# Layer 1's projection as seven products of quarters with spilled results, and one layout of buffers for a two-layer encoder

## The chip, the cores and the metric

The kernel runs on one core of a Trainium2 chip. The metric is device time in microseconds (us) of one execution. The engines are TensorE (PE: matmuls, with its weight loads shown as PEld), VectorE (DVE), ScalarE (ACT), GpSimd (POOL) and SyncE (SP, which here only issues DMAs). Sixteen DMA engines carry what SP and GpSimd issue.

## What is computed

Two post-norm layers on x of 512 tokens x 2048 features, in float32. Layer 1 is gated grouped-query attention with 16 query heads and 4 key/value heads of 128:

```python
proj = h @ w_in                                   # 2048 -> 5120: q 2048, k 512, v 512, g 2048
q = apply_rope(rms_norm(q, q_gain), cos, sin) * (A_HEAD_DIM ** -0.5)
k = apply_rope(rms_norm(k, k_gain), cos, sin)
...
p = jax.nn.softmax(s, axis=-1)                    # s = q k^T, per head, all 512 keys
...
return (o * jax.nn.silu(g)) @ w_out               # o = p v
```

Layer 2 is gated retention with 8 heads (q and k of 256, v and g of 512, so 2048 -> 12288): rope on q and k, scores times a decay by distance in both directions, times v, a norm per head, times silu(g), and an output projection 4096 -> 2048. After each layer x becomes layer_norm(ALPHA * x + y) with gain and bias.

## The kernel before

**Split products.** Every float32 operand is split into a rounded high part and a low part (`split`, L117: ACT copies the high part to fp32r, L118; DVE subtracts for the low part, L119). `mm3` (L261) is one product of 128x128 by 128x512 in three matmuls, high x high, high x low, low x high (L263 to L265). TensorE's order is the program's order. The other engines' orders come from the framework's planner, which schedules by data, buffers and its own costs.

**Weights** come in chunks of 128 x 1024 (512 KB), listed in `order` (L144). `load_chunk` (L233) issues the load through SP into a `raw` buffer and splits it; `next_chunk` (L250) keeps AHEAD = 2 chunks made ahead of the one in use. A `Stream` (L267) is a generator of products; `pump(us)` emits products worth so much by the constant MM3 (L274), so other work is placed between them by hand.

**Layer 1** (L586 to L605) goes group by group, four groups of four query heads with one k/v head. k and v of a group come from `kv_stream` (L474) as products of 256 columns, q from `q_stream` (L487) through `n_form` (L291), the gate from `gate_stream` (L496) through `t_form` (L307), which leaves features on the partitions. `q_group` does RMS norm and rope (`rms_open` L441, `rope` L452; two of its products are on GpSimd, L468) and turns q; `att_group` (L517) does scores, softmax (L527 to L532), transposes of the weights (L396), values, and the gate. The filler between those is the output projection of the group before (`out_proj`, L329), then the gate and the next k and v.

**Between the layers** `out_proj_last` (L343) works token tiles (0, 1), then 2, then 3; `norm_1` (L664) norms each and stores it to DRAM; `turn_1` (L672) transposes it and applies gain and bias on ACT. It is overlapped with products 1 and 2 of layer 2's first block (L805 to L813). Then the pools of layer 1 are closed and others opened (L815 to L817).

**Layer 2's projection** is done by seven products in place of eight: x is cut in quarters (token halves by feature halves), a block of weights (2048 x 1024) in four, and sums of quarters are multiplied (`form` L684 for x; `block_sum` L202 for the weights, whose sums DVE makes, L212). A product has four chunks; each chunk feeds four split products; a block is 7 x 4 x 4 = 112 split products, 336 matmuls. `evacuate` (L740) combines results, `deliver` (L722) applies rope or silu and stores to DRAM through GpSimd. There are 12 blocks, three for a pair of heads.

**Layer 2's heads.** `Head.run` (L896) does a head's scores and values, with the last block or the output projection of the head before as filler. After head 0 the pools change again (L987), and `residual` (L958) loads the normed layer-1 result and its gain and bias through GpSimd, multiplies on DVE and adds on GpSimd (L969, L970). `out_proj_last` with resident weights and `norm_2` (L927) end the kernel.

Of the kernel before, what the change touches and what calls it, by code (L numbers as in the profile page):

```python
# [26 lines left out]
N_G = R_HEADS // 2 * 3  # L27
CH = 1024
AHEAD = 2
ACC = 5  # L30
MM3 = 0.64
LOOK = 2
Q_HEAD = 7.0
Q_EACH = 4.5
A_HEAD = 2.0
EACH = 3.0
EACH_FIRST = 2.0
EACH_LAST = 2.0
PART = 0.5
T_HEAD = (4.0, 1.5, 4.0, 5.0)  # L40
T_EACH = 1.2
S_EACH = 1.2
S_TAIL = 2.0
O_EACH = 2.5
O_TAIL = 3.5
# [3 lines left out]
def encoder_trunk_kernel(  # L49
# [10 lines left out]

    nc = tc.nc
# [9 lines left out]
    class Pools:  # L71


        def __init__(self, **bufs):
            self.stack = ExitStack()
            for n, b in bufs.items():
                setattr(self, n, self.stack.enter_context(tc.tile_pool(name=n, bufs=b, reuse_waits="tile")))

        def close(self):
            self.stack.close()  # L80

    ph = Pools(hp=24, tmp=6, rp=3, yp=1)
# [7 lines left out]
    def bank():  # L90
        return psum.tile([P, 512], F32, tag="acc", name=nm("acc"))

    def bank2(name):
        return psum.tile([P, 512], F32, tag="att", name=nm(name), bufs=8 - ACC)

    def half(name, dt=F32R, tag="half"):
        return ph.hp.tile([P, 512], dt, tag=tag, name=nm(name), bufs=24 if tag == "half" else 4)

    def pair(name, tag="half"):
        return half(name + "h", F32R, tag), half(name + "l", F32R, tag)  # L100

    def temp(name):
        return ph.tmp.tile([P, 512], F32, tag="temp", name=nm(name))

    def unit(name, dt=F32R, pool=None):
        return (pool or xp).tile([P, 4, 512], dt, tag="x", name=nm(name))

    def small(name, n=1):
        return tiny.tile([P, n], F32, tag=name, name=nm(name))

    def v4(x):
        return x.rearrange("p (n d) -> p n d", d=P)

# [8 lines left out]
    def whole(hi, lo):  # L122
        return [(hi, lo, slice(0, 2))]

    def dest_stream(i):
        return whole(*[wp.tile([P, 2, 512], F32R, tag=n, name=nm(n)) for n in ("whi", "wlo")])

    def dest_halves(i):
        r = []
        for k in range(2):  # L130
            h, l = pair("ow", "sg" if i == n_l1 - 1 else "half")
            r.append((h.unsqueeze(1), l.unsqueeze(1), slice(k, k + 1)))
        return r

    resident = {}

    def dest_x(c, kc):
        def d(i):
            if kc == 0:
                resident[c] = [unit("wres") for _ in range(2)]  # L140
            return whole(*[m[:, 2 * kc:2 * kc + 2] for m in resident[c]])
        return d

    order = []  # L144

    def add(src, dest=dest_stream):
        order.append((src, dest))

    def add_n(w, u):
        for kc in range(8):  # L150
            add(w[u, kc])

    def add_t(w, u):
        for hf in range(2):
            add(w[u, hf])

    def add_o(w, u):
        for c in range(4):
            for kc in range(2):
                add(w[u, c, kc])  # L160

    def add_o_last(w, u, dest):
        for c in range(4):
            for kc in range(2):
                add(w[u, c, kc], dest(c, kc))

    for kc in range(4):
        add(a["wa_kv"][0, kc])
    for g in range(GROUPS):
        add_n(a["wa_q"], g)  # L170
        if g > 0:
            add_o(a["wa_o"], g - 1)
        for j in range(HPG):
            add_t(a["wa_g"], 4 * g + j)
        if g < GROUPS - 1:
            for kc in range(4):
                add(a["wa_kv"][g + 1, kc])
    add_o_last(a["wa_o"], GROUPS - 1, lambda c, kc: dest_stream if 2 * c + kc < 3 else dest_halves)
    n_l1 = len(order)
    FIRST = (1, 2, 5, 6, 3, 7, 4)  # L180
    PRODUCTS = (1, 5, 6, 3, 7, 2, 4)
    for g in range(N_G):
        for p in FIRST if g == 0 else PRODUCTS:
            for c in range(4):
                order.append((g, p, c))
        if g == 0:
            n_open = n_l1 + 8
    for h in range(R_HEADS - 1):
        add_o(a["wr_o"], h)
    add_o_last(a["wr_o"], R_HEADS - 1, dest_x)  # L190

    ready = []
    taken = [0]

    def raw_load(src):
        raw = ph.rp.tile([P, 2, 512], F32, tag="raw", name=nm("raw"))
        nc.sync.dma_start(out=raw.rearrange("p k n -> p (k n)"), in_=src)
        return raw

    held = {}  # L200

    def block_sum(g, p, c):  # L202

        def quarter(kh, nb):
            return raw_load(a["wr_in"][g, 2 * kh + nb, c])

        def keep(key, kh, nb):
            held[key, c] = quarter(kh, nb)
            return held[key, c]

        def onto(x, y):
            nc.vector.tensor_add(x, x, y)  # L212
# [882 lines left out]
```

## Time and profile before

| | |
|---|---|
| three runs | 2265.59, 2267.30, 2267.55 us; median 2267.3 |
| profiled execution | 2264.06 us, span of instructions 2262.3 us |
| PE, PEld busy | 2188.5 us (97%), 1830.5 us (81%) |
| DVE, ACT, POOL busy | 1590.7 us (70%), 956.8 us (42%), 204.0 us (9%) |
| TensorE instructions | 10448 |
| DMA | 300.66 MB, mean 133 GB/s |

The span runs from the first to the last instruction. Busy times of PE overlap, since matmuls are pipelined: a busy PE is not a full PE. A group's row gives line, engine, operation, output and inputs, shapes and count, then the busy time in us and the mean ns of one, then the idle time before it and what ended that. A row of the chain gives start, length, engine and line of one step. A row of the DMA issues gives count, size and the median us from issue to landing.

### The profile page before, as it was taken

The page shows a single profiled execution, that of the slowest core. Times are in us where ns is not written, and L with a number is a line of the kernel's source. Part 1 is how long each engine was busy: PE and PEld are TensorE (multiplying, and loading weights), DVE is VectorE, ACT ScalarE, POOL GpSimd, SP SyncE. Part 2 cuts the span into 40 slices and gives each one's busy share as a digit, 9 for nine tenths or more (in the row PEclk, how much of TensorE's full clock was granted, in tenths as well). Part 3 has the DMA queues.
Part 4 walks back from the last instruction along what each step waited for, and adds up shares of the span by engine and source line. Part 5 has one row for each costly group of instructions (what it writes and reads, how often), then busy time and mean ns, then how long its engine had stood idle before and what let it go on. Part 6 is the DMA issues. An engine that isn't in the chain of part 4 may idle for free.

```text
span 2262.3 us, 27514 instructions
## 1 busy us (share of the span) xinstructions
PE 2188.5 (97%) x10448; PEld 1830.5 (81%) x10448; DVE 1590.7 (70%) x2419; ACT 956.8 (42%) x1399; POOL 204.0 (9%) x247
## 2 busy tenths in 40 slices
PE   9999999999999979999999999999997699999997
PEld 8898888889888768888888888888886488888886
DVE  5565654655567897867787788778786766666667
ACT  4353243244245744444444444444464333333331
POOL 1201100200200000000000000000003400000004
PEclk9999999999999989999999999999999799999999
DMA  7312312322323364554465445545555433333332
GB/s 279 94 47 84 94 65 84 91 68 67 104 73 94 121 226 161 189 179 142 143 204 159 131 160 187 168 136 180 186 178 175 140 112 124 128 112 126 106 122 75
DMA packets 83557, 300.66 MB, mean 133 GB/s; under 512 B 10337, under 2 KB 11617, under 8 KB 81121
## 3 DMA queue, kind: packets, MB, share of 16 engines
q1 hardware_dynamic: 73440, 263.25, 36.0%
q0 software_dynamic: 9984, 35.66, 4.5%
q8 instruction: 82, 1.34, 0.2%
q14 instruction: 51, 0.41, 0.1%
HBM read 265.31 MB, written 33.55 MB: 132 GB/s over the span
## 4 chain that ended last, share of the span: by engine, by line
PE 91%; DVE 4%; POOL 2%; DMA 1%; issue 1%; ACT 1%; SPq 0%; POOLq 0%; DVEq 0%; ACTq 0%
PE acc L263 26%; PE acc L265 26%; PE acc L264 26%; PE tr L396 3%; PE o L263 2%; PE o L265 2%; PE o L264 2%; PE s L263 1%; PE s L264 1%; PE s L265 1%; POOL y L970 1%; DMA ln_bias<-in_ln_bias_dram 1%; DVE wlo L246 1%; DVE f L119 0%; DVE q_x L446 0%
## 5 line engine op out<-in xcount | busy, mean ns | idle before, releaser
L118 ACT CAST whi<-raw 128x1024 fp32r<-128x1024 f32 (+1 forms) x340 | 356.2, 1048 | 434.2 <-PE acc L265 393.2
L263 PE MATMUL acc<-whi,f 128*128 128x512 f32 x1344 | 526.1, 391 | 12.5 <-ACT whi L118 12.1
L264 PE MATMUL acc<-wlo,f 128*128 128x512 f32 x1344 | 523.9, 390 | 0.8 <-DVE wlo L119 0.7
L265 PE MATMUL acc<-whi,f 128*128 128x512 f32 x1344 | 523.7, 390 | 0.0
L119 DVE TENSOR_TENSOR wlo<-raw,whi 128x1024 fp32r<-128x1024 f32 (+1 forms) x340 | 409.5, 1212 | 154.0 <-ACT whi L118 149.8
L246 DVE TENSOR_TENSOR wlo<-raw,whi 128x512 fp32r<-128x512 f32 x324 | 215.2, 695 | 213.1 <-ACT whi L244 212.8
L244 ACT CAST whi<-raw 128x1024 fp32r<-128x1024 f32 x162 | 170.2, 1051 | 374.9 <-PE acc L265 192.2
L263 PEld LDWEIGHTS acc<-whi,f 128*128 128x128 f32 x1344 | 252.7, 188 | 65.1 <-ACT whi L118 12.5
L264 PEld LDWEIGHTS acc<-wlo,f 128*128 128x128 f32 x1344 | 252.8, 188 | 53.4 <-DVE wlo L119 1.9
L265 PEld LDWEIGHTS acc<-whi,f 128*128 128x128 f32 x1344 | 252.7, 188 | 52.6
L212 DVE TENSOR_TENSOR raw<-raw,raw 128x1024 f32<-128x1024 f32 x192 | 231.9, 1221 | 36.6 <-DMA raw<-in_wr_in_dram 35.5
L263 PE MATMUL acc<-whi,xT 128*128 128x256 f32 (+1 forms) x512 | 175.1, 342 | 4.9 <-ACT xT L118 4.9
L263 PE MATMUL acc<-whi,og 128*128 128x512 f32 x448 | 175.8, 392 | 0.0
L265 PE MATMUL acc<-whi,og 128*128 128x512 f32 x448 | 174.6, 390 | 0.0
L264 PE MATMUL acc<-wlo,og 128*128 128x512 f32 x448 | 174.6, 390 | 0.0
L265 PE MATMUL acc<-whi,xT 128*128 128x256 f32 (+1 forms) x512 | 173.6, 339 | 0.6 <-DVE xT L119 0.6
L264 PE MATMUL acc<-wlo,xT 128*128 128x256 f32 (+1 forms) x512 | 173.2, 338 | 0.0
L327 DVE TENSOR_TENSOR y<-acc,y 128x512 f32<-128x512 f32 x160 | 107.6, 686 | 26.7 <-PE acc L265 26.1
L263 PEld LDWEIGHTS acc<-whi,xT 128*128 128x128 f32 x512 | 98.3, 192 | 16.9 <-ACT xT L118 4.9
L265 PEld LDWEIGHTS acc<-whi,xT 128*128 128x128 f32 x512 | 98.2, 192 | 11.1 <-DVE xT L119 1.0
L264 PEld LDWEIGHTS acc<-wlo,xT 128*128 128x128 f32 x512 | 98.3, 192 | 10.1
L263 PE MATMUL acc<-xT,whi 128*128 128x512 f32 x256 | 102.6, 401 | 0.0
(184 smaller groups left out, 3355.8 us busy)
## 6 DMA issues: line engine op xcount, KB each, us to landing
raw<-in_wr_in_dram SPq DMA_DIRECT2D x248, 512.0 KB, 4.3
raw<-in_wr_o_dram SPq DMA_DIRECT2D x64, 512.0 KB, 3.6
raw<-in_wa_q_dram SPq DMA_DIRECT2D x32, 512.0 KB, 3.5
raw<-in_wa_g_dram SPq DMA_DIRECT2D x32, 512.0 KB, 3.5
raw<-in_wa_o_dram SPq DMA_DIRECT2D x32, 512.0 KB, 3.5
qkD<-qkT POOLq DMA_DIRECT2D x32, 256.0 KB, 5.4
vD<-t POOLq DMA_DIRECT2D x32, 256.0 KB, 5.0
raw<-qkD SPq DMA_DIRECT2D x16, 512.0 KB, 3.8
```

Source lines behind the costliest of these rows:

```text
L118: nc.scalar.copy(hi, src)
L119: nc.vector.tensor_sub(lo, src, hi.bitcast(F32))
L212: nc.vector.tensor_add(x, x, y)
L244: nc.scalar.copy(hi, raw[:, k])
L246: nc.vector.tensor_sub(lo[:, j], raw[:, k.start + j], hi[:, j].bitcast(F32))
L263: nc.tensor.matmul(ps, sh, mh, start=start, stop=False, skip_group_check=go_on)
L264: nc.tensor.matmul(ps, sh, ml, start=False, stop=False, skip_group_check=go_on)
L265: nc.tensor.matmul(ps, sl, mh, start=False, stop=stop, skip_group_check=go_on)
L327: nc.vector.tensor_add(yc, ps, yc)
L396: nc.tensor.transpose(out=b[:, tcols(i)], in_=src[:, tcols(i)], identity=ident)
L970: nc.gpsimd.tensor_add(y[:, t, cs], y[:, t, cs], gb[1])
```

## The change

Layer 1 becomes two stages. Its input projection is done like layer 2's: five blocks of two 512-column pieces, each by seven products of quarters, with all results spilled to DRAM. Attention then loads q, k, v and gate back, with the last block and later the output projections as filler. In the diff below, classes and functions that only changed their form are left out.

```diff
+A_COLS = ((("v", 0), ("g", 0)), (("g", 1), ("k", 0)), (("q", 0), ("q", 1)), (("q", 2), ("g", 2)), (("q", 3), ("g", 3)))
+FETCH = 3
-MM3 = 0.64
+MM3 = 0.68
+ORDER = (1, 5, 6, 3, 7, 2, 4)
...
-    xp = ctx.enter_context(tc.tile_pool(name="xp", bufs=8))
+    xp = ctx.enter_context(tc.tile_pool(name="xp", bufs=32))
+    rp = ctx.enter_context(tc.tile_pool(name="rp", bufs=9))
+    tmp = ctx.enter_context(tc.tile_pool(name="tmp", bufs=13))
-    psum = ctx.enter_context(tc.tile_pool(name="psum", bufs=ACC, space=bass.MemoryType.PSUM))
+    psum = ctx.enter_context(tc.tile_pool(name="psum", bufs=8, space=bass.MemoryType.PSUM))
...
+    def onto(x, src):
+        nc.gpsimd.dma_start(out=x, in_=src, accum_op=ALU.add)
...
+        def fetch(self, p, c):
...
+            if p == 1:
+                g[1 if self.first else "v", c] = raw_load(q(11))
+            elif p == 2:
+                g[2, c] = raw_load(q(21))
+            elif p == 6:
+                g[3, c] = raw_load(q(22))
+            elif p == 5 and self.first:
+                g["v", c] = raw_load(q(11))
+                onto(g["v", c], q(12))
+        def make(self, p, c):
...
+            if p == 6:
+                nc.vector.tensor_add(v, v, g[3, c])
+            elif p == 4 and not self.first:
+                nc.vector.tensor_add(v, v, g[2, c])
...
+        def follow(self, p, c):
...
+            if p == 1 and not self.first:
+                onto(g["v", c], q(12))
+            elif p == 3:
+                onto(g[3, c], q(12))
+            elif p == 6 and self.first:
+                onto(g["v", c], q(21))
...
+            fetch_to(len(ready) + 1 + FETCH)
+            make_chunk()
...
+        def out_proj_last(self, og):
+            for r in (0, 2):
+                for c in range(4):
...
+                            for t in (r, r + 1):
...
+    for ins, outs in ((a_in, a_out), (r_in, r_out)):
+        for b in ins[:2]:
+            b.add((1, 2))
+        for b in ins[:2]:
+            b.add((5, 6, 3, 7, 4))
+        for b in ins[2:]:
+            b.add(ORDER)
...
+        outs[-1].add(1)
...
+        for i in range(2):
-            nc.gpsimd.tensor_tensor(out=tv[:, :, :, i], in0=xv[:, :, :, 1 - i], in1=sb, op=ALU.mult)
+            nc.vector.tensor_tensor(out=tv[:, :, :, i], in0=xv[:, :, :, 1 - i], in1=sb, op=ALU.mult)
...
+    work = Stream(products(a_in[-1], x1, ORDER, ev1))
+    work.pump(31.5 * MM3)
...
+        attention(groups[g], groups[g + 1] if g + 1 < GROUPS else None, work, 2.2 if g else 2.7)
...
+    for c in range(4):
+        for t in range(NT):
+            hook(r_in[2 + c], (1, 6, 3, 2)[t], 2, residual_2, c, t)
...
-    ph.close()
-    ph = Pools(yp=1, tmp=8, rp=4)
-    residual()
+            total.load(lambda t: yD2[:, t])
...
-    nc = bacc.Bacc("TRN2", target_bir_lowering=False, num_devices=1, dynamic_dma_scratch_size=4096)
+    nc = bacc.Bacc("TRN2", target_bir_lowering=False, num_devices=1, dynamic_dma_scratch_size=2048)
```

- `Block.fetch` issues a chunk's loads FETCH chunks before it is made; `make` is its sum on DVE; `follow` is what is added to the quarter by an accumulating DMA from GpSimd (`onto`) once it is split. Of a regular block's 16 sums, eight stay on DVE and eight go to DMA; in the first two blocks of a layer four stay and twelve go to DMA.
- Both layers begin with products 1 and 2 of blocks 0 and 1, and then do the other five of each. Operand forms of x are made at hooks on chunks of those.
- Gate results now have tokens on the partitions. The reciprocal of the softmax sum is multiplied into the gate (one operation for four heads), which is then transposed (`Group.close`); the multiplication of each head's weights by it is gone.
- `out_proj_last` does token tiles 0 and 1, then 2 and 3, and streams the weights twice. Its norms come in pairs.
- `residual_2` makes the scaled residual of layer 2 during blocks 2 to 5 of its projection, 16 pieces, each loaded through SP, with two DVE operations, and stored through GpSimd; `Sum.load` loads the result (4 MB) after head 0.
- All pools live for the whole kernel; nothing is closed or opened between the stages.

More of the change, by code (lines that the diff above doesn't have):

```diff
@@ L250, in next_chunk, with fetch_to, make_chunk @@
+    def fetch_to(n):
+        while fetched[0] < min(len(order), n):
+            blk, p, c = order[fetched[0]]
+            blk.fetch(p, c)
+            fetched[0] += 1
+    def make_chunk():
+        blk, p, c = order[len(ready)]
+        raw = blk.make(p, c)
+        hi, lo = [wp.tile([P, CH], F32R, tag=n, name=nm(n)) for n in ("whi", "wlo")]
+        split(hi, lo, raw)
+        blk.follow(p, c)
+        ready.append([(half(hi, j), half(lo, j)) for j in range(2)])
     def next_chunk():
@@ L418, in start, with load_quarter @@
+    gD = [in_dram(f"gD{g}", [P, NT, 512]) for g in range(GROUPS)]
+    x1 = Operand()
+    def load_quarter(r, kh, i):
+        nc.sync.dma_start(out=x1.quarter(r, kh, i), in_=a["xq"][r, kh, i])
     def start():
[L420 to L421 removed]
+        blk = order[0][0]
+        raw = rp.tile([P, CH], F32, tag="raw", name=nm("raw"))
+        hi, lo = [wp.tile([P, CH], F32R, tag=n, name=nm(n)) for n in ("whi", "wlo")]
+        xf, (fh, fl) = x1.quarter(0, 0, 0), x1.new_form(1, 0)
@@ L507, in q_group @@
[L507 to L526 removed]
+        return dst, ss
@@ new lines, in attention @@
+            if w >= 0 and w % 2:
+                t, h = units[w]
+                g.values(h // 2, pT.pop(w))
+                if h == HPG - 1:
+                    g.weigh(t, p[w][1])
+            work.pump(each / 2)
+            if w >= 0 and w % HPG == HPG - 1:
+                g.close(w // HPG)
+    start()
+    ev1 = spill(deliver_1)
+    Stream(in_stream(a_in, x1, ev1, 1)).drain()
+    groups = [Group(g) for g in range(GROUPS)]
+    total = Sum()
+    work = Stream(products(a_in[-1], x1, ORDER, ev1))
@@ L813, in encoder_trunk_kernel @@
-    work.drain()
-    run_later(9)
-    ph.close()
-    f2 = ctx.enter_context(tc.tile_pool(name="f2", bufs=7, reuse_waits="tile"))
-    ph = Pools(rp=10, tmp=14)
-    form(5, 0)
-    form(5, 1)
-    Stream(group(0, FIRST[2:]), *[group(g) for g in range(1, N_G - 1)]).drain()
+                nc.scalar.copy(o, transpose4(m))
+                nc.gpsimd.dma_start(out=qkD[2 * pr + kind][:, :, tcols(t)], in_=v4(o))
+            turn_soon(lambda src: soon(3, put, rope_2(t, src)), t, src, own)
     def decay_strip(h):
-        st = const.tile([P, 896], F32, tag="tabs", name=nm("strip"))
+        st = const.tile([P, 1024], F32, tag="tabs", name=nm("strip"))
@@ new lines, in encoder_trunk_kernel @@
+    work = Stream(total.out_proj_last(groups[-1].out), in_stream(r_in, x2, ev2, 1))
+    work.until(lambda: 0 in total.rows)
+    norm_1(0)
+    norm_1(1)
+    work.pump(4.0)
+    for t in range(2):
+        for c in (0, 1, 2, 3):
+            turn_1(t, c)
+            work.pump(1.2)
+    work.until(lambda: 2 in total.rows)
+    norm_1(2)
+    norm_1(3)
+    work.pump(5.0)
+    for h in range(2):
+        for t in (2, 3):
+            for c in (h, h + 2):
+                turn_1(t, c)
+                work.pump(1.2)
+        x2.form(5, h)
@@ L1006, in encoder_trunk_kernel @@
-    ph.close()
+    heads[0].open()
+    work.pump(30.5 * MM3)
+    for h in range(R_HEADS):
+        if h:
+            work = Stream(total.out_proj(heads[h - 1].out, 1.0))
+        heads[h].run(work, heads[h + 1] if h + 1 < R_HEADS else None, 2.4)
+        work.drain()
+        if h == 0:
+            total.load(lambda t: yD2[:, t])
+    work = Stream(total.out_proj_last(heads[-1].out))
+    work.pump(20.0)
+    ln_params()
+    work.until(lambda: 0 in total.rows)
+    norm_2(0)
+    norm_2(1)
```

1102 lines of the change are left out of this document (482 added, 620 removed).

## The prediction

> **What bounds the kernel now.** I read the page's 40 slices first, then busy time by stretch, then the chain that ended last, then the groups of instructions by form and the DMA issues.
>
> ```profile
> span 2262.3 us, 27514 instructions
> ...
> PE   9999999999999979999999999999997699999997
> ```
>
> Of 40 slices TensorE is short of full in four: the 15th (791 to 848 us, the change of layers), two around 1700 to 1800 us, and the last. So the kernel is as long as its TensorE work plus what is lost there. The stretches (start and length; busy time with counts of PE, PEld, DVE, ACT, POOL; granted clock; DMA share; GB/s):
>
> ```profile
> 0.00:20.00 20.00, 14.53 (x93) 13.96 (x94) 12.60 (x24) 12.89 (x20) 0.20 (x4) 1.00 0.88 326
> 784.00:808.00 24.00, 7.41 (x25) 4.81 (x24) 24.00 (x32) 11.18 (x13) 1.46 (x2) 0.61 0.61 229
> 1089.00:1321.20 232.20, 232.20 (x1043) 192.45 (x1041) 182.50 (x199) 106.57 (x118) 14.54 (x24) 1.00 0.51 163
> 1739.00:1788.00 49.00, 14.35 (x43) 9.47 (x42) 34.43 (x34) 9.69 (x11) 28.96 (x21) 0.65 0.57 185
> ```
>
> Row 3 is one period of the retention projection: TensorE never stops, at clock 1.00. Rows 2 and 4 are the two places where it does: 24.00 - 7.41 = 16.6 us and 49.00 - 14.35 = 34.65 us idle, with the clock down to 0.61 and 0.65.
>
> The price of a matmul is its step in the chain, not its duration, since matmuls overlap:
>
> ```profile
> 1089.00 0.87 PE tr L396 x8
> ...
> 1321.22 0.87 PE tr L396 x8
> ```
>
> Between these lie 232.22 us, with three blocks of 336 products of 512 columns and four such runs of eight transposes. So a product costs (232.22 - 4 x 0.87) / 1008 = 0.227 us, a transpose 0.87 / 8 = 0.109 us, and a split product (three matmuls) 0.68 us; a chunk of weights feeds four of those, 2.72 us. In the k/v projection of layer 1, 256 columns wide, the chain shows
>
> ```profile
> 24.91 0.12 PE acc L263
> ```
>
> **The change part by part.** *Matmuls.* What layer 1's projection has now (one of three lines each):
>
> ```profile
> L263 PE MATMUL acc<-xT,whi 128*128 128x512 f32 x256 | 102.6, 401 | 0.0
> L263 PE MATMUL acc<-whi,xT 128*128 128x512 f32 x256 | 100.5, 392 | 0.0
> ...
> L263 PE MATMUL acc<-whi,xT 128*128 128x256 f32 x256 | 74.7, 292 | 4.9 <-ACT xT L118 4.9
> ```
>
> Removed: q and gate, 2 x 3 x 256 products of 512 columns (1536 x 0.227 = 348.5 us), and k/v, 768 x 0.12 = 92.2 us. Added: five blocks of seven products, 5 x 336 x 0.227 = 381.2 us, and 16 x 4 transposes of the gate, which now comes with tokens on the partitions, 64 x 0.109 = 7.0 us. Scores, values, the other transposes, the output projection and layer 2 keep their counts. Net -52.5 us, all on the path, since nothing but TensorE sets the pace there.
>
> *The change of layers.* Row 2 says who held TensorE: DVE is busy for 24.00 of 24.00 us. It makes most operand forms of layer 2 in one go, while only two products of one block are ready to cover that. After the change two blocks open with products 1 and 2: 32 more split products, 8 chunks x 2.72 = 21.8 us of cover, and no pool is closed in between. But the last output projection now reads its weights twice. The DVE groups and the cast:
>
> ```profile
> L119 DVE TENSOR_TENSOR wlo<-raw,whi 128x1024 fp32r<-128x1024 f32 x336 | 407.8, 1221 | 151.2 <-ACT whi L118 147.0 <-DMA raw<-in_wr_in_dram 3.5
> L118 ACT CAST whi<-raw 128x1024 fp32r<-128x1024 f32 x336 | 354.6, 1055 | 432.6 <-PE acc L265 393.2 <-issue 20.7 <-DVE raw L212 13.3
> ...
> L212 DVE TENSOR_TENSOR raw<-raw,raw 128x1024 f32<-128x1024 f32 x192 | 231.9, 1221 | 36.6 <-DMA raw<-in_wr_in_dram 35.5
> ...
> L327 DVE TENSOR_TENSOR y<-acc,y 128x512 f32<-128x512 f32 x160 | 107.6, 686 | 26.7 <-PE acc L265 26.1
> ...
> L366 DVE BATCH_NORM_STATS2 ln_st<-y 128x6 f32<-128x512 f32 x32 | 22.1, 690 | 0.7
> ```
>
> One pass over two token tiles is 8 chunks (21.8 us of TensorE) and costs DVE 8 x 1.221 + 8 x (0.686 + 0.690) = 20.8 us, before norms and turned operands, which on DVE come ahead of the next splits. Some stall must stay; I leave 8 of the 16.6 us (bounds 0 and 16.6). Gain 8.6.
>
> *Layer 2's projection to its output.* The chain through row 4:
>
> ```profile
> 1735.93 10.28 DMA ln_bias<-in_ln_bias_dram
> 1746.35 2.65 POOL y L970 x2
> 1749.56 11.13 POOL y L970 x6
> 1761.19 6.91 DMA ln_bias<-in_ln_bias_dram
> ```
>
> The residual is loaded, scaled on DVE and POOL, and only then used. The change makes it during four projection blocks: 16 pairs of DVE operations of about 0.7 us, 5.5 us a block, where row 3 shows DVE idle for 49.7 of 232.2 us. Its loads go through SP ahead of the next weights, its stores through GpSimd among the spills; both find their data ready. Only a plain load of 4 MB is left. At row 1's 326 / 0.88 = 370 GB/s that is 11.3 us, against 16 us until head 1 finishes its first output columns (4 score units of 6 x 0.227 us and 16 split products). I leave 4 us, for the buffers that come free with the last product (0 to 16). Gain 34.65 - 4 = 30.6.
>
> *DVE in layer 1.* Rope is wholly on DVE now, RMS first:
>
> ```profile
> L470 DVE TENSOR_TENSOR r_dst<-r_dst,r_sq 128x256 f32<-128x256 f32 x40 | 17.5, 468 | 2.5 <-POOL r_sq L468 2.5
> L457 DVE TENSOR_REDUCE r_ss<-r_sq 128x4 f32<-128x512 f32 x20 | 13.5, 674 | 0.0
> L469 DVE TENSOR_TENSOR r_dst<-q_x,tabs 128x256 f32<-128x256 f32 x32 | 12.7, 413 | 0.0
> ...
> L446 DVE SCALAR_TENSOR_TENSOR q_x<-acc,tabs 128x512 f32<-128x512 f32 x16 | 10.3, 684 | 6.6 <-ACT r_sq L445 6.6
> ```
>
> One tile: 0.684 + 0.674 + 4 x 0.413 + 2 x 0.468 = 3.95 us. The block of q0 and q1 delivers eight within 18 chunks: 31.6 us, with 18 splits (22.0), four sums (4.9) and four evacuations at 0.68 (2.7) 61.2 us, where TensorE needs 18 x 2.72 + 8 x 0.44 = 52.5. Two chunks made ahead are 5.4 us of lead; 3.3 are left: +3 (0 to 9).
>
> *Attention.* Two of its DVE groups now:
>
> ```profile
> L527 DVE TENSOR_REDUCE nmax<-s 128x1 f32<-128x512 f32 x64 | 44.0, 688 | 28.0 <-PE s L265 27.8
> L532 DVE TENSOR_SCALAR p<-p,rs 128x512 f32<-128x512 f32 x64 | 31.1, 486 | 2.0
> ```
>
> L532 goes (the weights are scaled through the gate). A unit then has L527 and a split of 512 columns, 0.69 as L327; a token tile has four more operations of that size. Beside the last block, group 0 runs 16 x 1.38 + 16 x 0.69 = 33.1 us of these, 20 weight splits (24.4), some six sums (7.3), four rope tiles (15.8) and six evacuations (4.1): 84.7 us. TensorE has 80 split products (54.4 us), 16 units of scores 0.68, transposes 4 x 0.109 and values 6 x 0.12 (29.4) and 8 turned tiles (3.5): 87.3. That is 97%, with order and latency on top: +4 (0 to 15; the high end takes in late PSUM banks, which now come from one pool of eight). In groups 1 to 3 the filler's chunk feeds eight split products in place of four, so DVE has room.
>
> The queues: q, gate, k and v come back through SP, ahead of the output weights; each waits for a temporary buffer, and the weights behind it have the nine raw buffers as lead. Layer 1's weight transfers grow from 80 to 116 and its spills by 40 stores and as many loads, 116 x 1.42 + 80 x 0.71 = 222 us of DMA as plain copies in some 680 us: hidden.
>
> *Sums of quarters by DMA.* Half of L212's additions go to accumulating DMAs issued by GpSimd, 512 KB each, and layer 1 adds its own. No accumulate is in the trace. The nearest rows:
>
> ```profile
> raw<-in_wr_in_dram SPq DMA_DIRECT2D x248, 512.0 KB, 4.3
> ...
> y<-yD POOLq DMA_DIRECT2D x4, 1024.0 KB, 10.7
> ```
>
> Call T the time per accumulate with all engines on it. Least: a plain copy, 524288 B / 370 GB/s = 1.42 us. Most: the slow GpSimd load, 10.7 / 2 = 5.35 us, with no overlap. The midpoint, 3.4, is what I take. Fixed latency is 4.3 - 1.42 = 2.9 us. Tightest is the first pair of blocks of each layer: 24 accumulates, 16 loads (22.7 us) and 8 spills of 256 KB (5.7) must be in within 40 chunks less a split, 108.8 - 2.3 = 106.5 us, the 2.3 being L118 and L119. So TensorE waits 24T - 78.1: 3.5 us a layer at 3.4, +7 for both. In a later block four accumulates queue between product 1 and product 5, issued 3.1 us ahead of product 1; the fourth is due 16.7 us after its start, so T up to 16.9 / 4 = 4.2 costs nothing. Queued behind a late one on GpSimd are the spills of finished tiles and RMS's power, which hold temporary buffers and only through those TensorE.
>
> The Trainium skill, "Collectives: The Full Stack", in its section on the bandwidth ceiling, says that an add in the DMA engine halves the rate because it reads two sources for each write, and that the add itself costs nothing. By it an estimate for T is 2 x 1.42 = 2.8 us, and the +7 would be 0; no run here shows it yet.
>
> *Start.* The first matmul:
>
> ```profile
> 4.88 0.58 PE L263 MATMUL acc<-whi,xT 128*128 128x256 f32 x1 [4.88 <-ACT xT L118]
> ```
>
> Until its fifth chunk the new order needs nine transfers of 512 KB: 4.72 MB at 326 GB/s is 14.5 us, with a split 16.8 and some issue time, 17.5, against 4.9 + 4 x 2.72 = 15.8 for TensorE: +2 (0 to 6).
>
> *End.* The last matmul starts at 2248.14, and DVE ends last:
>
> ```profile
> 2248.14 0.39 PE L265 MATMUL acc<-wres,og 128*128 128x512 f32 x1
> ```
>
> ```profile
> 2258.27 0.75 DVE y L941
> ```
>
> Now one token tile is normed after it, then two: 4 x 0.75 us and a reciprocal root, some 4 us; DVE's second pass (20.8 us plus two norms) adds 2. +6 (0 to 12).
>
> **Sum.** -52.5 - 8.6 - 30.6 + 3 + 4 + 7 + 2 + 6 = -69.7, a span of 2192.6. The profiled execution took 2264.06, 1.8 over its span, and the median 2267.3 is 3.2 above that: 2192.6 + 1.8 + 3.2 = 2198. Without the 22 of added stalls and the 12 left in the gaps it is 2164; with 11 more in attention, 6 in DVE's block and 6 at the end, 2221.
>
> **The rivals.** *The accumulating DMAs decide* (slower). At T = 5.35 the first pairs cost 2 x (128.4 - 78.1) = 100.6 us and each later block two bursts of 21.4 - 16.9 = 4.5 us, 26 in all, 117: 2198 - 7 + 218 = 2409. It is slower than before from 2(24T - 78.1) + 26(4T - 16.9) = 76, T = 4.4 us. For it: GpSimd's 10.7 us load, and that these sit between two splits. Against: that load was eight broadcast and residual loads at once. *DVE becomes the bound*: q block 8.7, attention 15, both last projections 5.4 each, in place of 3 and 4: 2198 + 28 = 2226. For: the 97% above. Against: row 3, where 182.5 of 232.2 us, 79%, goes with no wait. *The gaps stay*, other buffers late in place of the old: 2198 + 39 = 2237. For: 28 of 32 buffers hold operand forms until the last block. Against: the order of products frees them in fours.
>
> **How the numbers follow.** Forecast 0.66, DVE 0.13, gaps 0.10, accumulates 0.11. The first three are faster by over 0.2% (4.5 us, about what a measurement of this kernel can tell); I put 0.01 within it, where T is near 4.4. Range: 2160 to 2250 holds the first three; the accumulates and some of the mixed cases are out.
>
> **What would show it.** Right: 560 fewer TensorE instructions (2304 out, 1744 in) at an unchanged step; under 10 us of TensorE idle around the change of layers and under 5 before head 1, with no load or POOL operation in the chain there; accumulates that land in under 8 us. Wrong: TensorE waiting in every block for a split that waits for a DMA of raw, which is the accumulates; or for DVE, with DVE at 95% of layer 1's stretches; or as much idle in the two gaps as now.

## The result, and the profile after

| | before | after |
|---|---|---|
| median (four runs of each, on one chip) | 2267.43 us (2265.59 to 2270.92) | 2202.57 us (2198.51 to 2205.41) |
| profiled execution, span | 2264.06 us, 2262.3 us | 2198.51 us, 2196.6 us |

The ratio after / before is 0.9711, with a 95% interval of 0.9690 to 0.9732: faster by 65 us, where the forecast was 2198. The lines of the page of the changed kernel that answer to those shown of before:

```profile
span 2196.6 us, 26556 instructions
...
PE 2142.0 (98%) x9888; PEld 1767.6 (80%) x9888; DVE 1586.9 (72%) x2189; ACT 1043.4 (48%) x1365; POOL 341.5 (16%) x391
...
PE   8999999999999999999999999999999999999994
```

The two holes in the middle of TensorE's line are gone; its first slice and its last are poorer than before (8 and 4, where 9 and 7 stood). TensorE has 10448 - 9888 = 560 instructions fewer, as counted out beforehand. Busy time by stretch of the changed kernel (columns as in the prediction):

```profile
0.00:50.00 50.00, 42.12 (x160) 32.72 (x161) 32.23 (x34) 27.41 (x33) 4.97 (x10) 0.93 0.96 343
50.00:115.00 65.00, 63.50 (x277) 51.49 (x276) 51.83 (x62) 40.21 (x47) 17.81 (x20) 1.00 0.95 225
115.00:195.00 80.00, 77.22 (x346) 63.03 (x345) 59.15 (x80) 37.84 (x44) 24.38 (x24) 1.00 0.71 169
195.00:275.00 80.00, 77.98 (x355) 63.57 (x354) 63.59 (x103) 39.89 (x50) 31.35 (x22) 1.00 0.60 151
275.00:357.00 82.00, 81.62 (x368) 67.07 (x367) 64.67 (x90) 43.23 (x54) 36.24 (x22) 1.00 0.67 177
357.00:447.00 90.00, 88.66 (x476) 74.34 (x475) 75.54 (x123) 64.43 (x103) 12.54 (x13) 1.00 0.60 181
447.00:701.00 254.00, 253.50 (x1376) 215.41 (x1374) 188.79 (x329) 125.40 (x224) 4.85 (x7) 1.00 0.32 104
701.00:762.00 61.00, 56.76 (x271) 45.76 (x271) 58.87 (x102) 42.90 (x70) 9.07 (x14) 0.97 0.69 220
762.00:925.00 163.00, 160.16 (x719) 131.56 (x718) 120.75 (x141) 80.17 (x91) 34.54 (x44) 1.00 0.78 196
925.00:1050.00 125.00, 123.04 (x541) 100.65 (x540) 84.54 (x93) 58.17 (x65) 22.10 (x32) 1.00 0.77 209
1050.00:1627.00 577.00, 576.18 (x2581) 475.42 (x2580) 404.10 (x468) 275.53 (x315) 93.01 (x126) 1.00 0.66 171
1689.00:1800.00 111.00, 111.00 (x503) 91.83 (x502) 69.85 (x114) 42.24 (x59) 5.42 (x10) 1.00 0.48 163
2130.00:2196.60 66.60, 38.29 (x158) 30.58 (x156) 54.82 (x70) 16.74 (x18) 25.32 (x18) 0.82 0.25 88
```

Read column two against column one: what is missing is TensorE's idle time. The rows are, in order, layer 1's first two blocks (two rows and most of the third, to 173 us), its block with q0 and q1 (to 255 us) and the next one with the start of the last (to 357 us), attention's first group beside the last block, the other groups, the change of layers, the first pair of layer 2's blocks (to 892 us), its later blocks (two rows), head 0 and 1, and the end; two stretches in which TensorE is always busy (1627 to 1689 and 1800 to 2130 us) are left out. At head 1, where before lost 34.65 us, TensorE is busy for 111.00 of 111.00 us. The idle time now lies at the two ends of the kernel and in the change of layers, there 61.00 - 56.76 = 4.2 us in place of 16.6. The largest single wait is at the end (the group of TensorE's waits with the most time: total, times, longest):

```profile
PE acc L221 <- DVE wlo L105: 17.8, 12, 8.5
```

### The profile page after: what moved, and what is told of

Its sections match the earlier page's. It is cut to its first block, busy times and chain, and to the rows that moved or that the text cites. A ratio compares the mean times of both kernels' runs of the same rounds, so it can differ in the third digit from the quotient of the medians.

```text
span 2196.6 us, 26556 instructions
## 1 busy us (share of the span) xinstructions
PE 2142.0 (98%) x9888; PEld 1767.6 (80%) x9888; DVE 1586.9 (72%) x2189; ACT 1043.4 (48%) x1365; POOL 341.5 (16%) x391
## 4 chain that ended last, share of the span: by engine, by line
PE 82%; DVE 7%; DMA 4%; issue 3%; POOL 2%; ACT 1%; SPq 0%; POOLq 0%; ACTq 0%; DVEq 0%
PE acc L221 23%; PE acc L222 23%; PE acc L220 23%; PE tr L431 3%; DVE wlo L105 3%; DMA raw<-in_wa_in_dram 2%; PE o L220 2%; PE o L222 2%; PE o L221 2%; DMA raw<-in_wr_in_dram 2%; PE s L220 1%; PE s L222 1%; PE s L221 1%; ACT whi L104 1%; DVE f L105 1%
## 5 line engine op out<-in xcount | busy, mean ns | idle before, releaser
L105 DVE TENSOR_TENSOR wlo<-raw,whi 128x1024 fp32r<-128x1024 f32 (+1 forms) x589 | 716.9, 1221 | 362.2 <-ACT whi L104 355.4
L104 ACT CAST whi<-raw 128x1024 fp32r<-128x1024 f32 (+1 forms) x589 | 618.8, 1052 | 744.2 <-PE acc L222 651.4
L220 PE MATMUL acc<-whi,f 128*128 128x512 f32 x1904 | 750.5, 394 | 9.3 <-ACT f L104 4.5
L221 PE MATMUL acc<-wlo,f 128*128 128x512 f32 x1904 | 745.0, 391 | 6.6 <-DVE wlo L105 6.4
L222 PE MATMUL acc<-whi,f 128*128 128x512 f32 x1904 | 743.8, 391 | 0.7 <-DVE f L105 0.7
L220 PEld LDWEIGHTS acc<-whi,f 128*128 128x128 f32 x1904 | 358.6, 188 | 83.9 <-ACT whi L104 5.2
L222 PEld LDWEIGHTS acc<-whi,f 128*128 128x128 f32 x1904 | 358.3, 188 | 76.7 <-DVE f L105 1.6
L221 PE MATMUL acc<-wlo,ogh 128*128 128x512 f32 x768 | 301.3, 392 | 11.5 <-DVE wlo L105 11.5
L220 PE MATMUL acc<-whi,ogh 128*128 128x512 f32 x768 | 306.0, 398 | 0.5 <-ACT p L604 0.5
L222 PE MATMUL acc<-whi,ogl 128*128 128x512 f32 x768 | 301.0, 392 | 0.0
L221 PEld LDWEIGHTS acc<-wlo,ogh 128*128 128x128 f32 x768 | 145.5, 189 | 40.5 <-DVE wlo L105 12.7
L222 PEld LDWEIGHTS acc<-whi,ogl 128*128 128x128 f32 x768 | 145.2, 189 | 31.1
L604 ACT ACTIVATE p<-s,nmax,q_rs 128x512 f32<-128x512 f32 x64 | 50.0, 781 | 30.6 <-DVE nmax L602 28.2
```

The costliest lines, as they stand in the source:

```text
L104: nc.scalar.copy(hi, src)
L105: nc.vector.tensor_sub(lo, src, hi.bitcast(F32))
L220: nc.tensor.matmul(ps, sh, mh, start=start, stop=False, skip_group_check=go_on)
L221: nc.tensor.matmul(ps, sh, ml, start=False, stop=False, skip_group_check=go_on)
L222: nc.tensor.matmul(ps, sl, mh, start=False, stop=stop, skip_group_check=go_on)
L604: nc.scalar.activation(pt, sb, AF.Exp, scale=rs, bias=nmax, accum_out=self.sm[:, h:h + 1])
```

## The experiments

Each edit is to the changed kernel; each ratio is to the kernel before, from runs on the same chip. "Against the changed kernel" is the difference of the two ratios times 2267 us; with the intervals of both it is good to about 6 us.

**Is a matmul still worth its whole step?** In layer 1's blocks every product 4 is done a second time, into a bank that nothing reads.

```diff
+            again = bank("again") if p == 4 and op is x1 else None
...
+                        if again is not None:
+                            mm3(again, op.st(p, k, t), ks[j], c + j + t == 0, c == 3 and j + t == 2)
+                            yield MM3
```

> Layer 1's projection gets its 80 split products back: beside product 4 of each of the five blocks, 16 more split products go with the same operands into a PSUM bank that nobody reads; nothing else is added. Theory (only TensorE sets the pace in layer 1's projection, so the removed matmuls counted in full): 240 matmuls x 0.227 = 54 us more than the changed kernel, less some 5 us of its waits for DVE that the longer blocks absorb: 2248 to 2257 us. Rival (the projection is held by DVE or by the accumulating DMAs, and the matmuls were no longer the bound): under 35 us more, below 2238.

2253.71 us, ratio 0.9941 (0.9926 to 0.9956). The page's first line:

```profile
span 2250.2 us, 27034 instructions
```

The span grows by 53.6 us for 240 matmuls, 0.223 us each. So a matmul added to layer 1's projection is paid in full, and the price of 0.227 us, read in layer 2 and carrying the largest term of the sum, holds in the new stage.

**And a matmul less?** The third matmul (low x high) is left out of layer 1's projection, in 560 split products.

```diff
+    def mm2(ps, st, mv, start, stop, go_on=False):
...
-                        mm3(blk.bk[ch][t], ...)
+                        (mm2 if op is x1 else mm3)(blk.bk[ch][t], ...)
```

> Layer 1's projection leaves out the third matmul of each split product (low part of x times high part of the weights), 560 matmuls, so its output is less exact; all else stays. It asks how far TensorE is the bound there. By TensorE alone: 560 x 0.227 = 127 us less, 2076 us. Theory: DVE is next. In that stage DVE has 140 splits of 1.22 us, 32 sums of 1.22, 20 rope tiles of some 4 us, 20 evacuations of 0.7 and the operand forms, some 340 us against TensorE's 390, so the gain stops at about 50 us, 2140 to 2165 us, with DVE over 90% busy between 60 and 350 us.

2182.69 us, ratio 0.9633 (0.9618 to 0.9647). TensorE lost 560 x 0.227 = 127 us of work and the span shrank by only 2196.6 - 2179.7 = 16.9, where some 50 were expected. TensorE's waits in it (L226 and L227 are the products with two matmuls, L437 the transposes):

```profile
PE acc L227 <- DVE wlo L105: 24.0, 30, 1.8
PE tr L437 <- DVE r_dst L545: 18.5, 10, 3.6
...
PE acc L226 <- ACT whi L104: 12.4, 15, 2.4
```

One stretch of it:

```profile
195.00:275.00 80.00, 63.30 (x246) 47.03 (x245) 68.89 (x113) 39.96 (x51) 39.84 (x23) 0.90 0.59 155
```

Thirty waits for a split and ten for rope: the supply of split weights stands close behind TensorE. VectorE is busy for 68.89 of 80 us there, 86%, and not over the 90% that was expected; and the granted clock is 0.90 in place of 1.00, so that the matmuls that stay give back a part of what was saved. So the stage is bound by TensorE, but other limits follow some 17 us below, and a still smaller count of matmuls would have gained little.

**What if VectorE makes all sums of quarters?** The accumulating DMAs are replaced by plain loads through SP and additions on VectorE.

```diff
-                onto(g["v", c], q(12))
+                g["w", c] = raw_load(q(12))
...
+            if p == 5 or p == 4 and self.first:
+                nc.vector.tensor_add(v, v, g["w", c])
+            elif p == 7:
+                nc.vector.tensor_add(g[3, c], g[3, c], g["w", c])
```

> All sums of quarters go back to DVE: each accumulating DMA becomes a plain load through SP into a further raw buffer and an addition on DVE when the chunk is made; the nine raw buffers stay. 152 additions of 1.22 us, 186 us of DVE. Theory (the accumulates are hidden and buy DVE room where DVE is short): the retention blocks had these sums before at 79% DVE without a wait, so nothing there; in layer 1's blocks with rope, where DVE was near 100%, 8 to 15 us more; the first blocks gain at most 5: 2205 to 2218 us in all. Rival (the accumulates themselves hold TensorE, as waits for a split behind a DMA of raw): faster than the changed kernel, 2185 to 2195.

2233.5 us, ratio 0.9855 (0.9840 to 0.9870). The page's busy times, and the first two of TensorE's waits:

```profile
PE 2155.7 (96%) x9888; PEld 1776.0 (79%) x9888; DVE 1755.5 (79%) x2341; ACT 1041.8 (47%) x1363; POOL 221.3 (10%) x239
```

```profile
PE acc L225 <- DVE wlo L105: 30.8, 19, 8.5
PE acc L224 <- DVE t L339: 6.9, 4, 3.6
```

VectorE is busy for 1755.5 - 1586.9 = 169 us more and the time rises by some 33 us: the direction is right, the size twice the most that was expected. With all sums on VectorE half of the gain is gone. The place can be found because both traces hold the same 9888 TensorE instructions in the same order, so that the start of each can be compared: of the 38 us between the two profiled executions 22 are lost by 498 us of the changed kernel, in layer 1, 9 more by 1000 us, in layer 2's opening, nothing in the blocks from there to 1570 us, and 7 where head 0 starts. Each sum also holds one more of the nine `raw` buffers here; what share of the loss is that and what share VectorE's work isn't shown.

**Do the accumulates decide?** First try: before each accumulate, a plain copy of its source from DRAM to DRAM on the same queue.

```diff
     def onto(x, src):
+        for _ in range(1):
+            spare.append(in_dram(f"spare{len(spare)}", [P, CH]))
+            nc.gpsimd.dma_start(out=spare[-1], in_=src)
         nc.gpsimd.dma_start(out=x, in_=src, accum_op=ALU.add)
```

> Each of the 152 accumulating DMAs is preceded on GpSimd by a plain copy of the same 512 KB to a place in DRAM that nobody reads, so the time on the DMA engines per sum, T, goes from 2.9 us (two reads' worth, as the packets of the changed kernel's trace say) to about 4.3. By the rule of the prediction TensorE then waits 2 x (24 x 4.3 - 78.1) = 50 us in the first pairs and 26 x (4 x 4.3 - 16.9) = 8 us in the later blocks: 2245 to 2270 us. Rival (there is more room than the rule says, since the queues of SP and GpSimd overlap and buffers run ahead): under 15 us more, below 2218.

2318.79 us, ratio 1.0231 (1.0214 to 1.0248). This did not test what it was meant to. The copies wait for no data, and the planner put layer 2's copies into layer 1's stage, as busy time by stretch shows:

```profile
115.00:195.00 80.00, 72.56 (x302) 57.73 (x300) 41.19 (x50) 33.55 (x40) 29.77 (x43) 0.96 1.04 307
195.00:275.00 80.00, 70.38 (x291) 55.94 (x292) 52.97 (x73) 34.21 (x41) 36.53 (x51) 0.94 1.02 335
```

307 and 335 GB/s, where the changed kernel has 169 and 151, with the DMA engines at their limit; TensorE loses 7.4 and 9.6 us in 80. It tells only that layer 1's projection can't take twice its traffic without loss.

Second try: behind each of layer 2's accumulates, on its queue, a store of the sum that it has formed, which can't go early.

```diff
     def onto(x, src, more=False):
         nc.gpsimd.dma_start(out=x, in_=src, accum_op=ALU.add)
+        if more:
+            spare.append(in_dram(f"spare{len(spare)}", [P, CH]))
+            nc.gpsimd.dma_start(out=spare[-1], in_=x)
```

> Behind each of layer 2's 104 accumulating DMAs stands, on the same queue, a store of the tile that it has just formed (512 KB, to a spare place in DRAM that nothing reads), so that the queue carries one plain copy more for each accumulate and cannot do it early; layer 1 is left alone. Theory (the time on the queue for each accumulate decides, by the rule of the prediction): it goes from 2.9 us, twice the 1.42 us of a plain copy, to 4.3 us; the first pair of layer 2's blocks loses 24 x 4.3 - 78.1 = 25 us and its 10 later blocks two bursts each of 4 x 4.3 - 16.9 = 0.3 us, 6 us in all: about 31 us, 2225 to 2240, nearly all of the loss between 762 and 925 us. Rival (stores run beside the accumulates on engines that are idle, and hooks and queue order absorb them): under 10 us, 2203 to 2212.

2286.02 us, ratio 1.0079 (1.0066 to 1.0093): 83 us above the changed kernel, where 31 were expected. GpSimd's timeline shows what was overlooked (start, length, operation, idle time before it and what ended that; L118 is the accumulate, L121 the store):

```profile
783.08 0.88 POOL L118 DMA_DIRECT2D raw<-in_wr_in_dram  x1
789.99 0.55 POOL L121 DMA_DIRECT2D spare<-raw  x1 [6.03 <-DMA raw<-in_wr_in_dram]
790.62 0.87 POOL L118 DMA_DIRECT2D raw<-in_wr_in_dram  x1
...
797.58 0.56 POOL L121 DMA_DIRECT2D spare<-raw  x1 [4.55 <-DMA raw<-in_wr_in_dram]
```

GpSimd stands still until the accumulate has landed, 6.03 us, and all later accumulates and spills wait behind that: the accumulates run one or two at a time. From the first of these stores, at 763.20 us, to the twelfth, at 826.17, it is 62.97 / 11 = 5.7 us from one to the next, even above the T of 5.35 at which the slow rival was priced, here in layer 2 alone. It is a time of waiting, and not of busy DMA engines. The two groups of TensorE's waits with the most time are for splits:

```profile
PE acc L226 <- DVE wlo L105: 64.5, 44, 8.5
PE acc L225 <- ACT whi L104: 17.1, 7, 4.9
```

So this mechanism is real, and it can make the kernel slower than before; but the prediction's rule, 24 x 5.7 - 78.1 = 59 us for layer 2's first pair and 20 x (4 x 5.7 - 16.9) = 118 for its later blocks, would give 177 where 83 were measured: it overstates the cost by a factor of two. Nor does the loss lie nearly all in the first pair, as was expected: of the 89 us between the two profiled executions, matmul against matmul, 35 are lost by 965 us and the rest up to 1671 us.

Third try: what do they cost as they stand? They become plain loads, so the sums are left out and the result is wrong; everything else is left as it is.

```diff
-        nc.gpsimd.dma_start(out=x, in_=src, accum_op=ALU.add)
+        nc.gpsimd.dma_start(out=x, in_=src)
```

> All 152 accumulating DMAs become plain loads of the same size into the same buffers on the same queue: the sums of quarters are left out, so that products 5, 6, 7 and 4 take a wrong weight. Every wait, every issue and every instruction on the engines stays. Theory (accumulates cost the time nothing as they stand, and the 7 us that the prediction gave them was too much): T goes from 2.9 to 1.42 us, no stage after the opening changes by more than 1 us, the opening gains 0 to 3 us, 2198 to 2203. Rival (in the opening the DMA engines are busy to 0.95, and the accumulates' second reading is what keeps TensorE waiting there): the first 160 us lose 6 us or more less, 2190 to 2197.

2191.34 us, ratio 0.9660 (0.9647 to 0.9674), and a span of 2190.5, 6.1 below the changed kernel's. GpSimd's DMA queue on the page of the changed kernel, then of this one (packets, MB, share of 16 engines):

```profile
q0 software_dynamic: 35200, 123.75, 25.7%
```

```profile
q0 software_dynamic: 35200, 123.75, 16.9%
```

The same bytes take 0.257 x 2196.6 - 0.169 x 2190.5 = 194 us less of all sixteen engines, 1.28 us for each of the 152 accumulates. With 1.42 for a plain copy, T is 2.7 us. In the opening, from 50 us on, the DMA engines get free, and TensorE gains nothing:

```profile
0.00:50.00 50.00, 41.95 (x160) 33.06 (x161) 32.07 (x34) 27.23 (x33) 3.60 (x10) 0.93 0.96 357
50.00:115.00 65.00, 63.31 (x279) 51.78 (x278) 51.99 (x62) 40.38 (x47) 13.89 (x20) 1.00 0.64 227
```

DMA share 0.64 in place of 0.95 in the second row, and TensorE's busy time the same to 0.2 us in both. The time lies in the rival's range, but not for its reason: there is a gain, 6 us by the spans and about 12 by the medians, and it isn't in the opening. Matmul against matmul, 2.1 us of it come between 223 and 290 us, where the changed kernel's waits for rope (2.0 us in all) shrink to 1.1, and 3.6 between 940 and 1191 us, in layer 2's later blocks, where its waits for splits shrink from 2.6 to 1.4; the rest of the 12 is placed by no profile.

**The two gaps.** Layer 2 opens with one block instead of two:

```diff
-    r_in = [Block(a["wr_in"][g], g < 2) for g in range(R_G)]
+    r_in = [Block(a["wr_in"][g], g < 1) for g in range(R_G)]
...
-    for ins, outs in ((a_in, a_out), (r_in, r_out)):
-        for b in ins[:2]:
+    for ins, outs, m in ((a_in, a_out, 2), (r_in, r_out, 1)):
+        for b in ins[:m]:
```

> Layer 2 opens with products 1 and 2 of one block instead of two, so about 22 us less of TensorE's work lies ready while the first rows of layer 1's output are normalized and turned. Theory (the layer change shrank because the opening products cover it): the stretch from 701 to 762 us, in which TensorE lost 8.7 us, loses 17 to 25, and the time is 8 to 16 us above that of the changed kernel, 2210 to 2219. Rival (the old gap came from attention's last closing and from waits on GpSimd, and the new order of those removed it): the cover isn't needed, the time stays within 3 us of 2202.6.

2212.35 us, ratio 0.9755 (0.9741 to 0.9770), 10 us above the changed kernel, within what the theory of the cover gave. The same two stretches as above:

```profile
701.00:762.00 61.00, 53.10 (x248) 42.48 (x247) 53.55 (x98) 40.54 (x68) 10.55 (x16) 0.94 0.71 226
762.00:925.00 163.00, 157.68 (x695) 128.40 (x694) 124.51 (x148) 78.11 (x87) 27.87 (x36) 0.99 0.65 165
```

Idle time is 7.9 and 5.3 us where it was 4.2 and 2.8: the loss is spread over both, and the first doesn't lose the 17 to 25 us that were expected of it. The granted clock is also lower in both, 0.94 and 0.99 for 0.97 and 1.00.

The other: the residual is made after head 0 in one go, in the buffers of the sum.

```diff
-        f = temp("res")
-        nc.sync.dma_start(out=f, in_=nD[:, t, cs])
+        f = total.y[t, c]
...
-        nc.gpsimd.dma_start(out=yD2[:, t, cs], in_=f)
...
-            total.load(lambda t: yD2[:, t])
+            total.load(lambda t: nD[:, t])
+            for c in range(4):
+                for t in range(NT):
+                    residual_2(c, t)
```

> The residual of layer 2 is made in one go after head 0, in the buffers of the sum, as the kernel before did it, and not in small pieces beside the projection with a store and a load of its own. Theory (the gap of 34.65 us between layer 2's projection and its heads was this work): 32 VectorE operations of about 0.7 us, 22 us, and the loads that they wait for, some 11 us, come back in one block ahead of head 1; TensorE loses 10 to 30 us in 1690 to 1800 us, and the time is 2212 to 2232. Rival (the gap was the loads and splits of q and k for head 0, which the new order of buffers let start earlier): at most 5 us lost, 2203 to 2208.

2218.42 us, ratio 0.9781 (0.9766 to 0.9796), 16 us above the changed kernel. Its stretch, and the chain at that place, which has no TensorE in it from 1685.45 to 1724.28 us:

```profile
1689.00:1800.00 111.00, 95.34 (x410) 77.84 (x409) 78.05 (x128) 36.43 (x52) 3.80 (x7) 0.91 0.49 169
```

```profile
1685.45 13.82 DMA ln_gain<-in_ln_gain_dram
...
1699.30 1.29 DVE y L764 x2
...
1718.79 0.07 DVE y L765
```

The load of the gain, then VectorE's operations nearly back to back from 1699.3 to 1720.0, with 15.7 us of TensorE idle. So this work, done in one block, opens a gap there by itself, with no pool closed or opened. It is about half of the gap of before; that the rest was the additions on GpSimd and the loads through its queue, which this kernel hasn't got, is likely but not shown.

**The end.** It had taken more than its share, so four kernels go there. First, the last projection keeps its split weights in 16 buffers and does rows (0, 1), 2, 3, much as the kernel before did:

```diff
+        if blk is r_out[-1]:
+            hi, lo = x4("wres"), x4("wres")
...
+            for rows in ((0, 1), (2,), (3,)):
...
-    work = Stream(total.out_proj_last(heads[-1].out))
+    work = Stream(total.out_proj_kept(heads[-1].out))
```

> The last output projection runs over rows 0 and 1, then 2, then 3, and keeps its split weights in 16 buffers, so that they are loaded and split once and not twice. Theory (the end was mis-sized because the second pass over the weights puts eight more splits on VectorE in the midst of the first norms, and because two rows are left after the last matmul): the wait of 8.5 us for a split is gone, one row is left at the end in place of two, and the time falls by 8 to 15 us, to 2188 to 2195. Rival (the tail after the last matmul is a chain of one row's norm and stores, which stays): only the wait goes, 4 to 8 us, 2195 to 2199.

2189.19 us, ratio 0.9653 (0.9639 to 0.9668), 13 us below the changed kernel. The waits for splits, and the last matmul, in this kernel and then in the changed one:

```profile
PE acc L224 <- DVE wlo L105: 10.5, 10, 2.8
```

```profile
2164.85 0.39 PE L225 MATMUL acc<-wres,ogl 128*128 128x512 f32 x1
```

```profile
2176.55 0.39 PE L222 MATMUL acc<-whi,ogl 128*128 128x512 f32 x1
```

The wait of 8.5 us is gone and the last matmul comes 11.7 us earlier. What follows it shrinks only from 2196.6 - 2176.55 = 20.0 to 2182.9 - 2164.85 = 18.0 us, though one row is left there in place of two.

Second, in the changed kernel, rows 0 and 1 are normalized on VectorE alone:

```diff
-        own = 2 if t < NT - 1 else 3
+        own = 4 if t < 2 else 2 if t < NT - 1 else 3
```

> At the end, rows 0 and 1 are normalized on VectorE alone; GpSimd's four multiplies and four adds on them are gone. Theory (GpSimd's elementwise pieces slow VectorE beside them, 1.62 to 1.76 us for an operation that takes 0.74 alone and 2.3 us for a split of 1.22, and so delay the split for which TensorE waits 8.5 us): VectorE's operations on these rows go back to 0.74 us, eight more of them cost 6 us of VectorE, the wait of TensorE for the split at 2152 to 2161 us falls under 5 us, and the time falls by 3 to 6 us, to 2197 to 2200. Rival (VectorE simply has too much to do there): the eight added operations lengthen the wait, and the time rises by 2 to 6 us.

2199.49 us, ratio 0.9701 (0.9684 to 0.9717). By time alone this can't be told from the changed kernel. Matmul against matmul the end gains 3.0 us: up to 2150 us of the changed kernel each starts 5.0 us later here, after the wait 2.0 us later. The timelines of VectorE tell more; first the changed kernel, with GpSimd at its pieces from 2149.65 to 2163.54:

```profile
2149.30 0.74 DVE L926 SCALAR_TENSOR_TENSOR y<-y,mv,ln_gain 128x512 f32<-128x512 f32 x1
...
2156.76 1.75 DVE L926 SCALAR_TENSOR_TENSOR y<-y,mv,ln_gain 128x512 f32<-128x512 f32 x1
2158.44 2.28 DVE L105 TENSOR_TENSOR wlo<-raw,whi 128x1024 fp32r<-128x1024 f32 x1
...
2162.32 1.27 DVE L365 TENSOR_TENSOR y<-acc,y 128x512 f32<-128x512 f32 x2
```

and without these pieces:

```profile
2159.78 0.74 DVE L926 SCALAR_TENSOR_TENSOR y<-y,mv,ln_gain 128x512 f32<-128x512 f32 x1
2160.44 1.22 DVE L105 TENSOR_TENSOR wlo<-raw,whi 128x1024 fp32r<-128x1024 f32 x1
```

The same operation takes 0.74 us alone and 1.75 beside GpSimd, the split 1.22 and 2.28. The longest wait of TensorE for a split falls from 8.5 to 4.4 us, though VectorE has eight operations more. So the contention is real and is about half of that wait. The addition at 2162.32, which takes one of its inputs from a PSUM bank, runs beside GpSimd at 1.27 / 2 = 0.64 us and isn't slowed.

The Trainium skill, "SBUF — State Buffer", section "SBUF: two separate sides", says that VectorE and GpSimd share one pair of ports: an operation of VectorE with two inputs in SBUF and one of GpSimd that reads SBUF lock each other out for whole instructions. These rows agree: the slowed operations have two tensor inputs in SBUF, and the one that isn't slowed has one.

Third, both together, with rows 0 and 1 (`own` as above) or all four rows (`own = 4`) on VectorE.

> The last projection with kept weights, and rows 0 and 1 normalized on VectorE alone. Theory (both changes act on the same wait for a split, which the kept weights have already removed): nothing more is gained, 2186 to 2191, against 2189.2 with kept weights alone. Rival (GpSimd's pieces still slow the additions and statistics of the later rows): 3 to 5 us less, 2184 to 2186.

> The last projection with kept weights, and all four rows normalized on VectorE alone; GpSimd has only the powers left. Theory (in the tail of 17.7 us after the last matmul, GpSimd's pieces make VectorE's operations of 0.74 us take 1.63 to 1.75 and hold back the power of the next row on GpSimd's queue): the last row's eight operations take 5.5 us in one go, the power of row 3 no longer waits, and the time falls by 1 to 4 us against kept weights alone, to 2185 to 2188. Rival (VectorE then has 16 operations more, 11 us, between the last projection's additions): the additions come late and TensorE waits for banks, the time rises by 2 to 8 us.

2187.63 us, ratio 0.9645 (0.9632 to 0.9658), and 2188.65, ratio 0.9653 (0.9639 to 0.9666): neither can be told from kept weights alone. Where the kept weights have taken the wait, GpSimd's pieces cost nothing more that these runs can tell. In the second, where 1 to 4 us were expected, VectorE's operations on the last row do take 0.75 us again, but all eight of them are then VectorE's, and the end comes no sooner. The kernel with kept weights, in any of the three forms, is faster than both kernels of this case.

## Why the prediction was right

The span fell by 2262.3 - 2196.6 = 65.7 us; forecast were 69.7. The prediction read its gaps as idle time. That leaves something out: behind the long waits of these traces the granted clock was low for some us, and slow matmuls count as busy. In the changed kernel, behind the wait of 8.5 us at the end, matmuls start 0.43 us apart in place of 0.227, five of them in 2 us at a clock of 0.50:

```profile
2161.79 0.63 PE L220 MATMUL acc<-whi,ogh 128*128 128x512 f32 x1
2162.22 0.63 PE L221 MATMUL acc<-wlo,ogh 128*128 128x512 f32 x1
```

```profile
2161.00:2163.00 2.00, 2.00 (x5) 1.61 (x6) 2.00 (x3) 0.00 (x0) 1.92 (x2) 0.50 0.10 38
```

So what a stretch lost is counted here as what is left of it when each TensorE instruction in it is given its step, 0.227 us for 512 columns, 0.12 for 256 and 0.109 for a transpose. Term by term, from both traces:

- **Matmuls, -52.5.** Right: 560 fewer at an unchanged step, and the doubled product shows that the price holds in the new stage.
- **Change of layers, -8.6.** 7.3 us lost there and 4.2 in the first pair behind it, in place of 20.6 from 784 to 830 us before: -9.1. That the two opening blocks are its cover is shown by the kernel with one of them. One detail was wrong: the chain does hold GpSimd operations, such as the power of a later row's norm,

```profile
733.48 0.57 POOL rstd L414
```

- **Residual, -30.6.** 39.7 us from 1739 to 1800 before, 0.4 from 1689 to 1800 after: -39.3. The 4 us left for late buffers did not come, and what the gap loses beyond its idle time, 5 us, nearly all in slow matmuls, wasn't priced, though the row showed a clock of 0.65. Putting the work back in one block brought back 16 us, not 39; before, its additions ran on GpSimd as well.
- **DVE in the block of q0 and q1, +3, and attention, +4.** From 115 to 701 us 13.7 us are lost, where before lost 7.7 from 115 to 784: +6.0, with the accumulates' part in it. The block of q0 and q1 has four waits for rope of 2.0 us in all; the row from 115 to 195 us is idle for more, 2.8 us, but ahead of that block, in a wait for k's rope and one for a bank to be emptied. VectorE was busy beside attention's first group for 75.54 of 90 us, 84% and not 97%; so that rival had less ground than it seemed.
- **Accumulates, +7.** Right in size (6 by the spans, up to 12 by the medians), wrong in place and for the wrong reason. T is 2.7, not 3.4; with 2.7 the rule gives nothing for the first pairs, and indeed plain loads gain nothing there. By the rule T up to 4.2 costs nothing in the later blocks; that is the step that failed, for nearly all of the 6 us lies in those, 2.1 in layer 1 and 3.6 in layer 2. They land in 6.1 us (the median in layer 2), under the 8 that were named. The Trainium skill, "Collectives: The Full Stack", section on the bandwidth ceiling, halves the rate for an add. The estimate of 2.8 by it agrees with the 2.7 measured; the term would then have been 0, so that the midpoint came nearer to the 6 was luck. In layer 2's later blocks, the waits of the accumulates included, 6.9 us are lost from 925 to 1689, before 1.1 from 830 to 1700: +5.7.
- **Start, +2.** In the first 50 us before had 44.53 of 50 busy:

```profile
0.00:50.00 50.00, 44.53 (x273) 40.61 (x274) 28.26 (x54) 23.27 (x39) 3.54 (x7) 1.00 0.84 305
```

That is 5.5 us idle against 7.9, and the granted clock is 1.00 against 0.93. Up to 115 us 16.2 us are lost, before 9.3: +6.9, above the 6 that the prediction allowed.
- **End, +6.** This is the term that is off by most. After the last matmul 20.0 us pass in place of 14.2 (the span less the last matmul's start), +5.9, and ahead of it TensorE waits 8.5 us for a split and loses 2.7 more, nearly all in slow matmuls behind that wait: +17. The step that failed is "DVE's second pass adds 2": it priced VectorE's operations by their durations alone, where GpSimd's norms beside them double these, and it didn't ask what the split of the second pass stands behind on VectorE. The rule of the Trainium skill's page on SBUF, named above, would have said beforehand that these hold each other up. Keeping the weights brings 13 back.

Together -52.5 - 9.1 - 39.3 + 6.0 + 5.7 + 6.9 + 17.1 = -65.2, to set against -65.7. The mechanisms held, but that the sum came within 4 us is in part luck: the end took 11 us more than forecast and the start 5, and the residual gave 9 of that back, layer 1, the accumulates and the change of layers 3.

## What to carry to other kernels

Where TensorE never waits, a change is worth its matmuls by their step in the chain, and a gap is worth what covers it, with the slow matmuls behind it: find the engine that is full in the gap and move its work under a stage that has room. Ask then how near the next limit is, for in layer 1's projection it lay 17 us behind. At a kernel's end, price the operations of one engine with what runs beside them, and don't send weights through the same split twice where buffers to keep them are free.

## What the runs showed of the hardware

- Elementwise work on GpSimd slows operations of VectorE with two inputs in SBUF, from 0.74 to 1.75 us for 128x512 in float32 and from 1.22 to 2.28 for a split of 128x1024; without GpSimd's pieces both are short again.
- An accumulating DMA from DRAM into a `raw` buffer costs the DMA engines 2.7 us for 512 KB, about twice a plain copy (1.42), and lands 2.1 us later than a plain load on the same queue (median; the changed kernel, then the one with plain loads):

```profile
raw<-in_wr_in_dram POOLq DMA_DIRECT2D x104, 512.0 KB, 6.1
```

```profile
raw<-in_wr_in_dram POOLq DMA_DIRECT2D x104, 512.0 KB, 4.0
```

- A DMA issue on GpSimd that waits for data holds up everything behind it: with a store behind each accumulate it carried one every 5.7 us in layer 2's first blocks, where 6.1 us is the median landing time of one in the changed kernel.
- After the wait of 8.5 us at the end the granted clock was 0.50 until 2165 us and a matmul of 512 columns came every 0.43 us in place of 0.227.
